# Four of eight weight pairs of an FFN panel by seven products, with x kept in DRAM between the slices

## The chip, the cores and the metric

The kernel runs on one core of a Trainium2 chip. The metric is the device time of one launch in microseconds (us). A few engines of the core matter here: TensorE (PE, the matmuls), VectorE (DVE) and ScalarE (ACT), which prepare operands and clear results, GpSimd (POOL), which before the change does next to nothing, and SyncE (SP), whose queue issues the weight loads. PEclk in a row is the share of its full clock that TensorE was granted in that stretch.

## What is computed

The reference is a model of two layers on 256 tokens of width 2048, all in fp32: a hybrid layer (a Mamba-2 scan beside attention) and a second layer with a gated delta net and sparse attention. Each ends in a feed-forward network (FFN), and the change lies in these two:

```python
x = x + mixer(rmsnorm(x, g_mix))
h = rmsnorm(x, g_mlp) @ w_up          # [256, 2048] @ [2048, 8192]
h = relu(h) ** 2
x = x + h @ w_down                    # [256, 8192] @ [8192, 2048]
```

An FFN therefore reads 128 MB of weights, each of them once.

## The kernel before

The 256 tokens are two tiles of 128. A product with fp32 operands is done as three matmuls on halves of the mantissa: high by high, high by low, low by high. So each weight has to be split: ACT copies it rounded to `whi` (L281), DVE subtracts that from the weight and gets `wlo` (L282).

`wide` (from L243) multiplies a panel of 2048 rows by 1024 weight columns. It goes through the rows in eight **pairs** j = 0 to 7; a pair is 256 rows, one weight load of 1 MB into `wst` (three buffers). A pair that is not in `spairs` is **plain**: two splits of 1024 columns on ACT and DVE, 24 matmuls of 128x512. A pair in `spairs` is done by **seven products** of a block scheme (two token tiles by two row halves, two row halves by two column halves) instead of eight: 21 matmuls, in the order P1, P3, P5, P7, P6, P4, P2. For that DVE also forms differences of weight blocks, `t13` (L303) and `t24` (L306, L307), and the splits are of three and a half 1024-wide pieces: w11 and w22, t13, t24, w21. Splits go to pools `whp` and `wlp` with four buffers each, so a split of one piece waits until PE has finished the piece four earlier.

A panel's results lie in eight PSUM banks: P2, P3, P4 and E get the direct products, P1, P5, P6, P7 the shared ones. `shared` (from L326) turns the shared ones into the four parts that have to be added to the direct banks: a copy of P1 on ACT, then P6 + P1, P5 + that, P7 + that, P5 + that on DVE (L331 to L334), 128x512 each. The next call of `wide` swaps the two groups of banks, so its first products need the banks which L331 to L334 read.

`ffn` (from L402) works in four slices of 2048 hidden columns. A slice is four panels: two **up** panels (0 and 1), whose results go through relu and square (L416 to L418), transposes on PE (L430) and splits into `hT` (L170, L172), and two **down** panels (0 and 1). For the pairs done by seven products the activations need **forms**, sums of blocks of `hT` (L232 to L235) that are split again. Down results are added by `add_blocks` (L393 to L400) to x, which lies in four SBUF tiles `X` for the whole FFN. In the last slice the second down panel is two calls of `panel` (from L183, 512 columns, splits at L207 and L208), so that x is finished in pieces.

Before the change all these panels use

```python
SPAIRS = (2, 4, 6)
```

so a panel begins with two plain pairs and ends with a plain one. The instructions of each engine run in a fixed order, which a scheduler set when the program was built; an engine waits at an instruction until what it needs is there, and what follows in its order waits with it.

## Time and profile before

| | us |
|---|---|
| median of 3 runs | 2629.16 (2626.03 to 2631.44) |
| the profiled execution | 2627.97 |
| its span in the trace | 2626.2 |
| one slice of an FFN, in the middle of it | about 171 |
| PE busy in the span | 2595.7 (99%) |
| DVE busy | 2135.3 (81%) |
| ACT busy | 1496.7 (57%) |
| POOL busy | 42.0 (2%) |

The profiled execution took 1.8 us more than its span. The panels of the two FFNs lie at about 408 to 1140 and 1935 to 2626 us of the span. Matmuls overlap in the records (one lasts 0.39 us, the next starts 0.23 us after it), so the pitch, start to start, is what one costs; the same holds for DVE and ACT. In a row of the windows view the five busy times are those of PE, of its weight loads, of DVE, ACT and POOL.

### The profile page before, as it was taken

What the parts mean: (1) busy time and instruction counts of PE and PEld (TensorE: products, weight loads), DVE (VectorE), ACT (ScalarE), POOL (GpSimd) and SP (SyncE); (2) the same over time, 40 slices, a digit from 0 to 9 for tenths busy, and PEclk for the clock granted to TensorE, in tenths of its full rate; (3) what the DMA queues carried; (4) which work ended last, traced back from release to release, by engine and by line L of the source; (5) the groups of instructions that cost most, each with busy time, mean ns of one, the idle gap of its engine ahead of it and who ended that gap; (6) DMA issues with size and microseconds to landing.
All of it is one profiled execution on the core that took longest, in us unless ns stands there. A gap on an engine that the chain in (4) does not pass through costs nothing.

```text
span 2626.2 us, 32836 instructions
## 1 busy us (share of the span) xinstructions
PE 2595.7 (99%) x12521; PEld 2165.2 (82%) x12521; DVE 2135.3 (81%) x2966; ACT 1496.7 (57%) x2006; POOL 42.0 (2%) x46
## 2 busy tenths in 40 slices
PE   8999999999999999999999999999999999999998
PEld 8998887888888888888898887888778888888886
DVE  5767789999989999676755867588999999999995
ACT  5455456656657566554533655455667566565664
POOL 0000000000000000000000000000000000000000
PEclk9999999999999999999999999999999999999999
DMA  7454555565655656753432843556455556565554
GB/s 239 143 176 157 168 178 186 182 208 197 198 198 192 194 193 196 227 184 124 133 97 87 264 165 117 177 193 224 173 196 182 203 193 208 193 207 189 197 192 160
DMA packets 181916, 478.65 MB, mean 182 GB/s; under 512 B 9127, under 2 KB 50046, under 8 KB 181758
## 3 DMA queue, kind: packets, MB, share of 16 engines
q1 hardware_dynamic: 175600, 467.57, 53.5%
q10 hardware_dynamic: 6158, 8.99, 1.0%
q8 instruction: 98, 1.61, 0.2%
q14 instruction: 60, 0.49, 0.1%
HBM read 472.32 MB, written 4.21 MB: 181 GB/s over the span
## 4 chain that ended last, share of the span: by engine, by line
PE 92%; DVE 4%; ACT 1%; DMA 1%; issue 1%; ACTq 0%; POOL 0%; POOLq 0%; SPq 0%; DVEq 0%
PE mm L270 25%; PE tp L270 13%; PE sx L270 12%; PE mm L194 10%; PE mm L193 10%; PE mm L192 10%; DVE wlo L282 2%; DMA wst<-in_w_down_dram 1%; PE sx L1021 1%; PE sx L1016 1%; ACT whi L281 1%; PE mm L430 1%; PE tp L915 0%; PE tp L369 0%; PE sx L1300 0%
## 5 line engine op out<-in xcount | busy, mean ns | idle before, releaser
L281 ACT ACTIVATE whi<-wst 128x1024 fp32r<-128x1024 f32 (+1 forms) x560 | 542.8, 979 | 312.9 <-PE mm L270 127.5
L282 DVE TENSOR_TENSOR wlo<-wst,whi 128x1024 fp32r<-128x1024 f32 (+1 forms) x560 | 615.8, 1120 | 66.1 <-ACT whi L281 63.8
L208 DVE TENSOR_TENSOR wlo<-wst,whi 128x1024 fp32r<-128x1024 f32 (+6 forms) x336 | 377.3, 1128 | 207.6 <-ACT whi L207 206.5
L207 ACT ACTIVATE whi<-wst 128x1024 fp32r<-128x1024 f32 (+6 forms) x336 | 329.2, 983 | 323.4 <-PE mm L194 294.1
L281 ACT ACTIVATE whi<-t 128x1024 fp32r<-128x1024 f32 x210 | 222.1, 1057 | 261.3 <-DVE t L307 117.0
L282 DVE TENSOR_TENSOR wlo<-t,whi 128x1024 fp32r<-128x1024 f32 x210 | 256.3, 1222 | 49.4 <-ACT whi L281 47.1
L193 PE MATMUL mm<-wlo,x2h 128*128 128x512 f32 (+3 forms) x608 | 228.3, 376 | 1.7 <-DVE wlo L208 1.7
L194 PE MATMUL mm<-whi,x2l 128*128 128x512 f32 (+3 forms) x608 | 229.7, 378 | 0.0
L192 PE MATMUL mm<-whi,x2h 128*128 128x512 f32 (+3 forms) x608 | 228.3, 376 | 0.0
L192 PE MATMUL mm<-whi,xnh 128*128 128x512 f32 (+3 forms) x416 | 152.4, 368 | 2.0 <-ACT whi L207 1.6
L270 PE MATMUL mm<-wlo,xnh 128*128 128x512 f32 x392 | 153.6, 392 | 0.4 <-DVE wlo L282 0.3
L270 PE MATMUL mm<-whi,xnl 128*128 128x512 f32 x392 | 153.1, 391 | 0.0
L270 PE MATMUL mm<-whi,xnh 128*128 128x512 f32 x392 | 151.4, 391 | 1.3 <-ACT whi L281 1.3
L193 PE MATMUL mm<-wlo,xnh 128*128 128x512 f32 (+3 forms) x416 | 151.7, 365 | 0.0
L194 PE MATMUL mm<-whi,xnl 128*128 128x512 f32 (+3 forms) x416 | 150.6, 365 | 0.1
L303 DVE TENSOR_TENSOR t<-wst 128x1024 f32<-128x1024 f32 x105 | 128.2, 1221 | 15.6 <-DMA wst<-in_w_down_dram 11.3
L270 PE MATMUL mm<-wlo,hTh 128*128 128x512 f32 x343 | 134.3, 392 | 0.8 <-DVE wlo L282 0.8
L270 PE MATMUL mm<-whi,hTl 128*128 128x512 f32 x343 | 133.6, 390 | 0.0
L270 PE MATMUL mm<-whi,hTh 128*128 128x512 f32 x343 | 132.0, 390 | 0.0
L193 PEld LDWEIGHTS mm<-wlo,x2h 128*128 128x128 f32 x608 | 114.7, 189 | 17.1 <-DVE wlo L208 2.0
L194 PEld LDWEIGHTS mm<-whi,x2l 128*128 128x128 f32 x608 | 114.5, 188 | 15.3 <-issue 1.0
L192 PEld LDWEIGHTS mm<-whi,x2h 128*128 128x128 f32 x608 | 114.7, 189 | 15.0 <-issue 0.8
(614 smaller groups left out, 5695.7 us busy)
## 6 DMA issues: line engine op xcount, KB each, us to landing
wst<-in_w_up_dram SPq DMA_DIRECT2D x128, 1024.0 KB, 5.0
wst<-in_w_down_dram SPq DMA_DIRECT2D x128, 1024.0 KB, 5.3
wst<-in_w_in_dram SPq DMA_DIRECT2D x84, 1024.0 KB, 5.1
wst<-in_w_out_dram SPq DMA_DIRECT2D x16, 1024.0 KB, 5.5
wst<-in_w_o_dram SPq DMA_DIRECT2D x16, 1024.0 KB, 5.2
wst<-in_w_in_dram SPq DMA_DIRECT2D x16, 780.0 KB, 4.5
wst<-in_w_in_dram SPq DMA_DIRECT2D x12, 824.0 KB, 4.5
wst<-in_w_in_dram SPq DMA_DIRECT2D x12, 736.0 KB, 6.2
```

Source lines behind the costliest of these rows:

```text
L192: PE.matmul(ps[t][:, :n], xh[:, sl], wa, start=kt == first, stop=False)
L193: PE.matmul(ps[t][:, :n], xh[:, sl], wb, start=False, stop=False)
L194: PE.matmul(ps[t][:, :n], xl[:, sl], wa, start=False, stop=kt == last)
L207: S.activation(a[:, :2 * n], src, AF.Copy)
L208: V.tensor_tensor(b[:, :2 * n], src, a[:, :2 * n].bitcast(F32), op=OP.subtract)
L270: PE.matmul(B[b], x, y, start=left[b] == total[b], stop=left[b] == 1)
L281: S.activation(a[:, :n], src, AF.Copy)
L282: V.tensor_tensor(b[:, :n], src, a[:, :n].bitcast(F32), op=OP.subtract)
L303: V.tensor_tensor(t13, s.rearrange("p (k l n) -> p k l n", k=2, l=2)[:, :, 0], s[:, :1024].rearrange("p (l n) -> p l n", l=2)[:, ::-1], op ...
L430: PE.transpose(pv[:, kk, t, :], us[t, l][:, c:c + 128], ident)
L1016: PE.matmul(ps[:, i * 64:(i + 1) * 64].rearrange("p (m b) -> p m b", b=b), N[:, i], half(T[:, i], 0), start=True, stop=True)
L1021: PE.matmul(ps[:, i * 64:(i + 1) * 64].rearrange("p (m b) -> p m b", b=b), P[:, i], half(Tt[:, i], 1), start=True, stop=True)
```

## The change

A second set of pairs is brought in. A panel that follows a down panel (up panel 0 of slices 1 to 3, down panel 1 of slices 0 to 2) does pairs 1, 3, 5 and 7 by seven products; the other `wide` panels of an FFN do 3, 5 and 7. x no longer stays in SBUF: it is written to DRAM (`xd`) at the FFN's start, and in the slices 0 to 2 the parts (`ca`, `cb`) and ACT's copies of the direct banks (`cd`) are added to it by DMAs issued from POOL that accumulate, four of 512 KB for a down panel. In slice 3 x is loaded back and DVE adds to it as before. The forms are now four for a slice, not three.

```diff
-    SPAIRS = (2, 4, 6)
+    SPAIRS, NPAIRS = (2, 4, 6), (1, 3, 5, 7)
...
+    def part_pairs():
+
+        return sp([128, 2, 512], name="ca"), s4([128, 2, 512], name="cb")
+
...
         for s_ in range(4):
             hT, hforms = [], {}
             for P in range(2):
-                B, tags = wide(w_up, 0, s_ * 2048 + P * 1024, at_k(act), forms, spairs=SPAIRS,
+                B, tags = wide(w_up, 0, s_ * 2048 + P * 1024, at_k(act), forms,
+                               spairs=NPAIRS[1:] if r is None or P == 1 else NPAIRS,
                                hooks={2: hook} if r is None else {})
                 us = {}
-                for i, l, part, bank in shared(B):
+                for i, l, part, bank in shared(B, part_pairs()):
...
-                        if j in SPAIRS:
-                            f = two_forms()
+                        if j in NPAIRS:
+                            f = two_forms(sp)
...
             for P in range(2):
+                if s_ == 3:
+                    for p in (2 * P, 2 * P + 1):
+                        X[p] = sp([128, 2, 512], name=f"X{p}")
+                        nc.scalar.dma_start(X[p], xd[:, p])
...
-                B, _ = wide(w_down, s_ * 2048, P * 1024, at_k(hT), hforms)
-                add_blocks(B, P)
+                B, _ = wide(w_down, s_ * 2048, P * 1024, at_k(hT), hforms, spairs=NPAIRS[1 - P:])
                 if s_ == 3:
+                    add_blocks(B, P, part_pairs())
                     for p in range(2):
                         for t in range(2):
                             after(p, t)
+                    continue
+                pairs = part_pairs()
+                out_ = shared(B, pairs)
+                banks = []
+                for l in range(2):
+                    d = sp([128, 2, 512], name="cd")
+                    for i, l_, part, bank in out_:
+                        if l_ == l:
+                            S.activation(d[:, i], bank, AF.Copy)
+                    banks.append(d)
+                for src in (pairs, banks):
+                    for l in range(2):
+                        G.dma_start(xd[:, 2 * P + 1 - l], src[l], accum_op=OP.add)
```

The lines shift by some seven to ten: L331 to L334 become L334 to L337, L397 and L400 become L404 and L407, L416 becomes L424.

Two places show what this does to the engines' orders. The first is DVE at the end of down panel 0 of the last slice in the first FFN, where `panel` follows. `wlo` at L208 is the first low half that `panel` needs; X0 and X1 are two tiles of x. Before:

```order
L331 TENSOR_TENSOR cu2_9036<-mm1_8801,cp1_9035 128x512
L208 TENSOR_TENSOR wlo_9103<-wst_9100,whi_9102 128x1024
L332 TENSOR_TENSOR cu4_9037<-mm0_8800,cu2_9036 128x512
L208 TENSOR_TENSOR wlo_9119<-wst_9100,whi_9118 128x1024
L333 TENSOR_TENSOR cu2_9036<-mm1_8802,cu2_9036 128x512
L397 TENSOR_TENSOR X0_2971<-cu4_9037,X0_2971 128x512
L334 TENSOR_TENSOR cv_9038<-mm0_8800,cu2_9036 128x512
L397 TENSOR_TENSOR X1_2972<-cu2_9036,X1_2972 128x512
L397 TENSOR_TENSOR X0_2971<-cv_9038,X0_2971 128x512
L400 TENSOR_TENSOR X1_2972<-tp_8725,X1_2972 128x512
```

After the change, on the same engine at the same place (`tp_8827` is the bank P2, the last that the panel's seven-product pair fills):

```order
L335 TENSOR_TENSOR cb_9138<-mm0_8936,ca_9137 128x512
L407 TENSOR_TENSOR X1_8825<-tp_8827,X1_8825 128x512
L336 TENSOR_TENSOR ca_9137<-mm1_8938,ca_9137 128x512
L404 TENSOR_TENSOR X0_8823<-cb_9138,X0_8823 128x512
L337 TENSOR_TENSOR cb_9138<-mm0_8936,ca_9137 128x512
L404 TENSOR_TENSOR X1_8825<-ca_9137,X1_8825 128x512
L404 TENSOR_TENSOR X0_8823<-cb_9138,X0_8823 128x512
L407 TENSOR_TENSOR X0_8823<-tp_8828,X0_8823 128x512
L407 TENSOR_TENSOR X1_8825<-sx_8829,X1_8825 128x512
L407 TENSOR_TENSOR X0_8823<-sx_8830,X0_8823 128x512
L208 TENSOR_TENSOR wlo_9207<-wst_9204,whi_9206 128x1024
```

The first two splits for `panel` stood among the sums before; now the first stands behind all of them, nine instructions after P2 is first read (that one included).

The second place is the first seven-product pair of a panel that follows an up panel, here down panel 0 of slice 2 in the first FFN. On DVE, `t13_7393` and `t24_7395` are the weight sums of that pair (pair 2). Before:

```order
L282 TENSOR_TENSOR wlo_7409<-t13_7393,whi_7408 128x1024
L172 TENSOR_TENSOR sfl_7279<-ff_7270,sfh_7278 128x512
L235 TENSOR_TENSOR ff_7296<-ff_7296 128x128
L172 TENSOR_TENSOR hTl_7290<-ff_7296,hTh_7289 128x512
L172 TENSOR_TENSOR hTl_7290<-mm1_7308,hTh_7289 128x512
L172 TENSOR_TENSOR sfl_7305<-ff_7296,sfh_7304 128x512
L282 TENSOR_TENSOR wlo_7419<-t24_7395,whi_7418 128x1024
```

After, on DVE, where that pair is pair 3 (`t13_7499`, `t24_7501`), and `t13_7577` belongs to pair 5:

```order
L306 TENSOR_TENSOR t24_7501<-wst_7493,t13_7499 128x512
L282 TENSOR_TENSOR wlo_7505<-wst_7493,whi_7504 128x1024
L172 TENSOR_TENSOR sfl_7384<-ff_7375,sfh_7383 128x512
L307 TENSOR_TENSOR t24_7501<-wst_7493,t24_7501 128x512
L282 TENSOR_TENSOR wlo_7515<-t13_7499,whi_7514 128x1024
L303 TENSOR_TENSOR t13_7577<-wst_7575 128x1024
L282 TENSOR_TENSOR wlo_7525<-t24_7501,whi_7524 128x1024
```

One more 1024-wide sum, the `t13` of the pair after next, now stands ahead of the low half of `t24`. On PE the matmuls of the same pair, after the change, from P5 on (`mm0_7496` is P5, `mm1_7498` P7, `mm1_7497` P6):

```order
L270 MATMUL mm0_7496<-whi_7514,sfh_7002 128x512
L270 MATMUL mm1_7498<-whi_7514,sfh_7002 128x512
L270 MATMUL mm1_7497<-whi_7524,sfh_7002 128x512
L270 MATMUL mm0_7496<-wlo_7515,sfh_7002 128x512
L270 MATMUL mm0_7496<-whi_7514,sfl_7003 128x512
L270 MATMUL mm1_7498<-wlo_7515,sfh_7002 128x512
L270 MATMUL mm1_7498<-whi_7514,sfl_7003 128x512
L270 MATMUL sx_7389<-whi_7524,hTh_6980 128x512
L270 MATMUL tp_7387<-whi_7534,hTh_6980 128x512
L270 MATMUL tp_7388<-whi_7543,hTh_7335 128x512
L270 MATMUL sx_7390<-whi_7543,hTh_7335 128x512
L270 MATMUL mm1_7497<-wlo_7525,sfh_7002 128x512
```

The first matmul on the low half of `t24` (the last row) is the eighteenth matmul of its pair; before the change it was the fifteenth.

## Rows read from the trace of the kernel before

**Rows 1.** The page: busy time of the engines, and the chain by engine
```profile
PE 2595.7 (99%) x12521; PEld 2165.2 (82%) x12521; DVE 2135.3 (81%) x2966; ACT 1496.7 (57%) x2006; POOL 42.0 (2%) x46
...
PE 92%; DVE 4%; ACT 1%; DMA 1%; issue 1%; ACTq 0%; POOL 0%; POOLq 0%; SPq 0%; DVEq 0%
```

**Rows 2.** Windows, one slice each: stretch, length, busy (instructions), PEclk, DMA share, GB/s
```profile
453.00:625.00 172.00, 171.72 (x769) 140.63 (x768) 158.44 (x189) 103.83 (x122) 0.00 (x0) 1.00 0.60 198
...
2184.50:2355.00 170.50, 170.25 (x765) 140.12 (x764) 157.24 (x188) 104.34 (x122) 0.00 (x0) 1.00 0.57 198
```

**Rows 3.** Chain in order of time: start, length, what, how many
```profile
2294.54 6.80 PE mm L270 x30
```

**Rows 4.** Timeline, first up panel, first FFN, PE: start, length, what, [idle before <-releaser]
```profile
418.35 0.40 PE L270 MATMUL tp<-whi,sfh 128*128 128x512 f32 x1
420.32 0.73 PE L270 MATMUL mm<-whi,sfh 128*128 128x512 f32 x2 [1.57 <-DVE sfl L172]
422.07 0.50 PE L270 MATMUL mm<-whi,sfh 128*128 128x512 f32 x1 [1.01 <-ACT whi L281]
...
426.09 0.40 PE L270 MATMUL mm<-whi,sfl 128*128 128x512 f32 x1
```

**Rows 5.** Windows of that place, and of the last panels of the second FFN
```profile
417.50:426.20 8.70, 6.11 (x19) 4.12 (x19) 7.83 (x12) 4.96 (x7) 1.07 (x1) 0.80 0.02 9
...
2572.50:2576.50 4.00, 4.00 (x13) 3.10 (x12) 3.10 (x5) 1.36 (x5) 0.00 (x0) 0.57 0.79 261
```

**Rows 6.** Timeline, first up panel of the second FFN, PE
```profile
1941.50 0.50 PE L270 MATMUL mm<-wlo,xnh 128*128 128x512 f32 x1 [0.29 <-DVE wlo L282]
```

**Rows 7.** Timeline, up panel to down panel, slice 2, first FFN, DVE
```profile
832.20 1.23 DVE L282 TENSOR_TENSOR wlo<-wst,whi 128x1024 fp32r<-128x1024 f32 x1 [1.09 <-ACT whi L281]
...
841.54 2.35 DVE L282 TENSOR_TENSOR wlo<-wst,whi 128x1024 fp32r<-128x1024 f32 x2
843.80 1.22 DVE L303 TENSOR_TENSOR t<-wst 128x1024 f32<-128x1024 f32 x1
...
854.17 1.22 DVE L282 TENSOR_TENSOR wlo<-t,whi 128x1024 fp32r<-128x1024 f32 x1
```

**Rows 8.** The same place, PE
```profile
829.55 0.39 PE L270 MATMUL tp<-whi,xnh 128*128 128x512 f32 x1
...
852.62 0.39 PE L270 MATMUL mm<-whi,hTh 128*128 128x512 f32 x1
...
855.79 0.39 PE L270 MATMUL mm<-wlo,sfh 128*128 128x512 f32 x1
```

**Rows 9.** Timeline, down panel to up panel, first FFN, PE
```profile
586.81 0.50 PE L270 MATMUL mm<-whi,xnh 128*128 128x512 f32 x1 [0.24 <-ACT whi L281]
```

**Rows 10.** Timeline, end of down panel 0, slice 3, first FFN, DVE
```profile
1052.83 1.22 DVE L208 TENSOR_TENSOR wlo<-wst,whi 128x1024 fp32r<-128x1024 f32 x1
...
1056.96 1.28 DVE L400 TENSOR_TENSOR X<-tp,X 128x512 f32<-128x512 f32 x2
```

**Rows 11.** The same place, PE
```profile
1055.09 0.39 PE L192 MATMUL mm<-whi,hTh 128*128 128x512 f32 x1
```

**Rows 12.** Timeline, the same end in the second FFN, DVE
```profile
2571.01 2.48 DVE L400 TENSOR_TENSOR X<-mm,X 128x512 f32<-128x512 f32 x4
```

**Rows 13.** The same place, PE
```profile
2568.89 0.39 PE L270 MATMUL mm<-whi,hTl 128*128 128x512 f32 x1
...
2571.85 0.47 PE L192 MATMUL mm<-whi,hTh 128*128 128x512 f32 x1 [2.57 <-DVE X L400]
...
2572.85 0.54 PE L193 MATMUL mm<-wlo,hTh 128*128 128x512 f32 x1
...
2576.18 0.48 PE L192 MATMUL mm<-whi,hTh 128*128 128x512 f32 x1
```

**Rows 14.** DMA issues: tile<-source, queue, kind, how many, KB each, median us to landing
```profile
wst<-in_w_down_dram SPq DMA_DIRECT2D x128, 1024.0 KB, 5.3
...
xsave<-X ACTq DMA_DIRECT2D x4, 512.0 KB, 5.6
```

More of the change, by code (lines that the diff above doesn't have):

```diff
@@ L219, in panel, with two_forms @@
         return ps
-    SPAIRS = (2, 4, 6)
+    SPAIRS, NPAIRS = (2, 4, 6), (1, 3, 5, 7)
     turn = [0]
-    def two_forms():
-        f = s4([128, 2, 512], name="ff")
+    def two_forms(pool=s4):
+        f = pool([128, 2, 512], name="ff")
         return f[:, 0].rearrange("p (k t c) -> p k t c", k=2, t=2), f[:, 1].rearrange("p (f c) -> p f c", f=4)
@@ L325, in wide, with shared @@
         return B, ka
-    def shared(B):
-        p1, u2, u4, v = (s2([128, 512], name=n) for n in ("cp1", "cu2", "cu4", "cv"))
+    def shared(B, pairs=None):
+        if pairs is None:
+            p1, u2, u4, v = (s2([128, 512], name=n) for n in ("cp1", "cu2", "cu4", "cv"))
+        else:
+            (p1, u2), (u4, v) = ((t[:, 0], t[:, 1]) for t in pairs)
         S.activation(p1, B["P1"], AF.Copy)
@@ L369, in x_to_act @@
                     PE.transpose(ps[:, kk, t, :], x[:, t, (k0 + kk) * 128:(k0 + kk + 1) * 128], ident)
-            if forms is not None and 2 * p + k0 // 2 in SPAIRS:
+            if forms is not None and 2 * p + k0 // 2 in NPAIRS:
                 f = two_forms()
@@ L391, in flat, with add_blocks @@
         return ap.rearrange("p k c -> p (k c)")
-    def add_blocks(B, P):
-        out_ = shared(B)
+    def part_pairs():
+        return sp([128, 2, 512], name="ca"), s4([128, 2, 512], name="cb")
+    def add_blocks(B, P, pairs=None):
+        out_ = shared(B, pairs)
         for i, l, part, bank in out_:
@@ L400, in add_blocks, with ffn @@
             V.tensor_tensor(x, bank, x, op=OP.add)
-    def ffn(act, forms, w_up, w_down, late, after, tail=0):
+    def ffn(act, forms, xd, w_up, w_down, late, after, tail=0):
         r = None
@@ L451, in ffn @@
                             after(p, t)
+                    continue
+                pairs = part_pairs()
+                out_ = shared(B, pairs)
+                banks = []
[8 more added lines that the diff above has]
+                        G.dma_start(xd[:, 2 * P + 1 - l], src[l], accum_op=OP.add)
     ssx = tiny([128, 2, 4], "ssx", bufs=2)
@@ L824, in x_done @@
             sumsq(ssx[:, t, p:p + 1], X[p][:, t])
+        nc.scalar.dma_start(xd[:, p], X[p])
     X = x_panels()
     xforms = {}
+    xd = drp.tile([128, 4, 2, 512], F32, name="xd")
     for p in range(4):
@@ L852, in after1 @@
             nc.scalar.dma_start(xsave[:, p], X[p])
-    ffn(xn, xforms, I["w_up"][0], I["w_down"][0], late1, after1)
+    ffn(xn, xforms, xd, I["w_up"][0], I["w_down"][0], late1, after1)
     if upto == 2:
@@ L1376, in build @@
     xforms = {}
+    xd = drp.tile([128, 4, 2, 512], F32, name="xd2")
     ssx = tiny([128, 2, 4], "ssx", bufs=2)
@@ L1416, in after2 @@
         nc.sync.dma_start(o[:, 1024:1536], X[2][:, t])
-    ffn(xn, xforms, I["w_up_2"][0], I["w_down_2"][0], late2, after2, tail=8)
+    ffn(xn, xforms, xd, I["w_up_2"][0], I["w_down_2"][0], late2, after2, tail=8)
 _INS = ["x", "g_mix", "w_in", "conv_w", "conv_b", "dt_bias", "a_log", "d_skip", "g_ssd", "g_q", "g_k", "g_kidx",
```

## The prediction

> **What bounds the kernel now.** I read the page first: PE is busy for 99% of the span and makes up 92% of the chain, DVE is next with 81% [rows 1]. In the middle of an FFN it is tighter still: PE is busy for 171.7 of 172.0 us at full clock, DVE for 158.4, ACT for 103.8, and the DMA engines are used to 0.60 [rows 2]. So two things follow. Matmuls taken away are time taken away, one for one, where nothing else becomes late. And little more than the matmuls can be gained inside a slice, since PE stands still for under 1 us in it; whereas DVE, with 13 us to spare in 171, can become late at any place where its work is bunched. The question is therefore not the load of DVE but what stands in its order ahead of a half that PE needs.
>
> Prices, all pitches: a matmul 6.80/30 = 0.2267 us [rows 3]; a 1024-wide DVE operation 1.13 (two in 2.35, one alone 1.22) [rows 7]; a 512-wide one 0.60 (four in 2.48, two in 1.28) [rows 10, 12]. A plain pair is then 24 x 0.2267 = 5.44 us of PE and 2.26 of DVE; a pair by seven products 4.76 of PE and 4 x 1.13 + 3 x 0.60 = 6.3 of DVE.
>
> **Matmuls removed.** Six panels of each FFN have four instead of three such pairs: 2 x 6 x 3 = 36 matmuls fewer, 36 x 0.2267 = **-8.2 us**, all on the path.
>
> **DVE's load.** A slice gets two more such pairs (2 x 4.0 = +8), loses sixteen additions to x (-9.6) and gains one form (about +1.4). It stays near 157 us. So what counts is the places.
>
> **First up panels.** In the first up panel of an FFN the first pair by seven products was 2 and is now 3, so 5.44 us of plain work cover the wait for its form. Now PE waits 1.57 us for the form and 1.01 for a high half [rows 4], and the clock is 0.80 over the stretch [rows 5]: from 418.35 to 426.09 thirteen matmuls start, worth 2.9 us, so 4.8 are lost. In the second FFN a wait of 0.29 is marked [rows 6], with some more around it. DVE has one more form to make ahead of it. I take 2 and 1: **-3 us**, bounds -1 and -6.
>
> **Up panel to next panel** (sixteen times). All panels of an FFN done by `wide` now end with pair 7 by seven products, and a panel after an up panel then has three plain pairs and pair 3. Before, it was pair 6, plain 7, 0, 1 and pair 2: the same PE work from one such pair to the next, 852.62 - 829.55 = 23.1 us [rows 8]. DVE starts this stretch 2.65 us after the pair's start (832.20) and is never idle for long until the low half of `t24` at 854.17 + 1.22 = 855.39 [rows 7]; PE uses that at 855.79 [rows 8]. It is on time by 0.40 us. After the change the list from the first shared sum to that half is the same, sixteen 512-wide and eight 128-wide operations, but ten 1024-wide ones and not nine (`t13` of pair 5 is put ahead): +1.13. PE's order for its part uses the half three matmuls later, +0.68 of cover. Late by 1.13 - 0.40 - 0.68 = 0.05 us. That is the floor: the three matmuls moved ahead need high halves from ACT at that moment, and every bubble in DVE's chain (transposes, copies, forms, handed to and fro with ACT and PE) now comes on top, without slack. If the cover doesn't work it is 0.73, with bubbles 0.9. I take 0.4: 16 x 0.4 = **+6.4 us**, bounds 0 and 14.
>
> **Down panel to next panel** (twelve times). The next panel's products need the banks that the four shared sums read; a plain pair 7 used to cover these. Now, from the start of pair 7: 2.65 us to DVE's first split, then three 1024-wide and five 512-wide operations to the last sum, 2.65 + 3.4 + 3.0 = 9.05. PE has 4.76 of pair 7 and, with P2 and P4 of pair 0 put first and E next, 18 matmuls (4.1) ahead of P3, 8.84: late by 0.2 to 0.4. The gap there now is 0.24 as marked [rows 9]. Net 0.12 each, **+1.5 us**, bounds 0 and 4. The sixteen fewer additions to x lie behind these sums and free nothing earlier. ACT's 48 copies of direct banks and the splits behind them fit in its 68 idle us of a slice [rows 2]; I cost them at nothing, and at 0.5 us each where ACT is late, which the upper bound holds.
>
> **End of down panel 0 in slice 3** (once in each FFN). Here DVE still adds to x, and `panel` comes next. Before, its first low halves were made between the sums (1052.83), the additions of banks came later (1056.96) [rows 10], and PE went on at 1055.09 with no idle marked [rows 11]. Now nine 512-wide additions and sums stand between the first reading of P2 and `wlo`. P2 is complete 4.76 us after the start of pair 7, read from 4.96: 4.96 + 9 x 0.60 = 10.4, with the split 11.5. PE has done 4.76 + 0.45 by then, and 0.9 of transposes of x that it has to do anyway: it waits 5.4. In the second FFN it waits already: from 2568.89 + 0.23 to 2571.85, 2.7 us, for the additions [rows 12, 13]. There the low half comes one operation later still, 12.1: a wait of about 6.9, so +4.2. After its wait that place ran at 0.57 of the clock [rows 5]: eight matmuls in 3.33 us and not 1.81, 1.5 lost [rows 13]; the first FFN gets that new, the second perhaps 0.4 more. 5.4 + 4.2 + 1.5 + 0.4 = **+11.5 us**, bounds 7 (the sums start early, no loss of clock) and 15 (a longer low clock).
>
> **Accumulating DMAs.** The trace has none. A down panel's four of 512 KB are 2 MB beside 8 MB of weights. A copy of 512 KB from SBUF to DRAM lands in 5.6 us, a load of 1 MB in 5.3 [rows 14]. At the price of plain bytes the share rises from 0.60 [rows 2] to 0.75, and the three weight buffers hide it; full it is at 2.7 times that price. Nothing on POOL waits behind them, and their sources are needed again 25 us and more later (by the panel lengths). Value 0, bounds 0 and the third rival.
>
> The Trainium skill has a rule that speaks against this: "Collectives: The Full Stack", section "The bandwidth ceiling: the fold count and why AG ≠ RS ≠ AR", says that an adding transfer reads two sources for each write, and gives 32 against 62 GB/s. By that rule the share here would be about 0.90 (an estimate), which leaves the sum as it is but brings the third rival near; no run here shows it yet.
>
> **The sum**: -8.2 - 3 + 6.4 + 1.5 + 11.5 = +8.2. The profiled execution took 2627.97 us, so 2636.2; the median of the three runs is 1.2 above it, within their spread of 5. I predict 2636.
>
> **Rivals.** (1) *Not slower: DVE stays ahead after every panel.* PE's later use of the low halves suffices, and both transition terms are 0: 2628.0 - 8.2 - 3 + 11.5 = 2628. For it: 0.05 us is all that the count shows. Against: no slack is left. It decides at 0.1 us of bubbles in a transition. (2) *Faster: the wait in slice 3 is short as well*, because DVE takes up most sums before P2 is complete: its lower bound 7, the first up panels' full 6, no transition cost: 2628.0 - 8.2 - 6 + 7 = 2621. For it: the same sums were started early before (1052.83) [rows 10]. Against: PE completes P6 and P2 only at the panel's end now. (3) *The additions fill the DMA engines.* At three times the price of plain bytes the share in a down panel would be 0.60 x 1.75 = 1.05, so 5% of 43 us, 2.1 us for each of twelve: 2636 + 26 = 2662; at four times 2740. For it: the weights in the same engines. Against: 0.40 is free.
>
> **How the numbers follow.** Chances: forecast 0.53, (1) 0.27, (2) 0.10, (3) 0.10. The sum of all lower bounds is -8, of all upper ones +24; so 2621 to 2652, with a little for the third rival 2654. A measurement of this kernel tells about 0.2%, 5.3 us, from no change. Faster than that: rival 2 and the edge of 1, 0.12. Within: most of 1 and the low side of the forecast, 0.28. Slower: 0.60.
>
> **What would show it.** PE's busy time down by about 8 us. In slice 3 a wait of some 5 us for `wlo` of L208 in the first FFN and some 7 in the second, each followed by matmuls at 0.43 us. After up panels, waits of 0.1 to 0.9 us for `wlo` from `t24` in pair 3; slices near 171 us still. DMA share near 0.68 in the slices 0 to 2. Wrong it would be if slices were shorter by 1.4 us and the two ends cost nothing, or if weight loads became what DVE and ACT wait for.

## The result: slower by 2.3%, and where the time went

| kernel | median, us | ratio to the kernel before (95% interval) | profiled span, us |
|---|---|---|---|
| before | 2629.16 (2626.03 to 2631.44, 5 runs) | | 2626.2 |
| after | 2688.22 (2685.22 to 2692.92, 5 runs) | 1.0226 [1.0214, 1.0237] | 2684.5 |

Slower was forecast, but by 8, not by 59; the time lies outside the range of 2621 to 2654.

The page of the changed kernel first: its span, the busy times, the share of each engine in the chain of work that ended last, the queue of DMAs issued from POOL (packets, MB, share of 16 engines' span), and some DMA issues (count, KB each, median us to landing; the last two lines are from the DMA view).

```profile
span 2684.5 us, 33032 instructions
PE 2612.6 (97%) x12485; PEld 2153.5 (80%) x12485; DVE 2138.8 (80%) x2978; ACT 1555.9 (58%) x2098; POOL 82.6 (3%) x94
...
q0 software_dynamic: 6912, 25.17, 5.3%
...
PE 63%; DVE 20%; DMA 9%; ACT 5%; issue 3%; ACTq 0%; POOL 0%; POOLq 0%; DVEq 0%; SPq 0%
...
wst<-in_w_up_dram SPq DMA_DIRECT2D x128, 1024.0 KB, 5.1
wst<-in_w_down_dram SPq DMA_DIRECT2D x128, 1024.0 KB, 5.5
...
xd<-cd POOLq DMA_DIRECT2D x24, 512.0 KB, 10.1
...
xd<-ca POOLq DMA_DIRECT2D x12, 512.0 KB, 6.7
xd<-cb POOLq DMA_DIRECT2D x12, 512.0 KB, 8.3
```

PE made up 92% of the chain before [rows 1] and makes up 63% now; DVE and the DMAs stand where it stood. DVE does hardly more than before. The weight loads land in the same median time as before [rows 14], which hides a few that take twice as long. An adding DMA of 512 KB takes 6.7 to 10.1 us in the median.

A slice of the first and one of the second FFN, as in [rows 2] (us, the five busy times, PEclk, DMA share, GB/s):

```profile
618.20:797.30 179.10, 173.37 (x758) 138.02 (x758) 156.84 (x187) 112.83 (x137) 6.92 (x8) 1.00 0.69 212
...
2165.20:2342.00 176.80, 172.43 (x758) 138.27 (x758) 156.94 (x187) 113.07 (x137) 6.92 (x8) 1.00 0.68 215
```

A slice took 172.0 and 170.5 and takes 179.1 and 176.8, at full clock and with the DVE load that the prediction gave (157). PE now stands still for 4 to 6 us of it. The mean DMA share of 0.69 looks harmless.

To see which panels pay, take the start of each panel's first matmul from the trace of the profiled execution, and the time to the next one. Means in us; the last two columns run from the start of down panel 0 of slice 3 to the next layer's first `wide` panel (first FFN) and to the last matmul (second FFN):

| | after a down panel (12) | up panel 1 (8) | down panel 0 (6) | first up panels (2) | end, FFN 1 | end, FFN 2 |
|---|---|---|---|---|---|---|
| before | 42.10 | 43.50 | 43.47 | 48.13, 46.33 | 693.7 | 91.6 |
| after | 44.07 | 45.07 | 45.22 | 43.47, 44.17 | 701.2 | 101.1 |
| difference, all | +23.7 | +12.6 | +10.5 | -6.8 | +7.5 | +9.5 |

That is +57.0 of the +58.3 of span. The panels after a down panel are the surprise: three matmuls fewer should have made them 0.68 shorter, and they are 1.97 longer.

### The profile page after: what moved, and what is told of

It is laid out like the page before. It is cut to its first block, busy times and chain, and to the rows that moved or that the text cites. A ratio compares the mean times of both kernels' runs of the same rounds, so it can differ in the third digit from the quotient of the medians.

```text
span 2684.5 us, 33032 instructions
## 1 busy us (share of the span) xinstructions
PE 2612.6 (97%) x12485; PEld 2153.5 (80%) x12485; DVE 2138.8 (80%) x2978; ACT 1555.9 (58%) x2098; POOL 82.6 (3%) x94
## 3 DMA queue, kind: packets, MB, share of 16 engines
q0 software_dynamic: 6912, 25.17, 5.3%
## 4 chain that ended last, share of the span: by engine, by line
PE 63%; DVE 20%; DMA 9%; ACT 5%; issue 3%; ACTq 0%; POOL 0%; POOLq 0%; DVEq 0%; SPq 0%
PE mm L270 12%; PE mm L194 10%; PE mm L193 10%; PE mm L192 10%; DVE wlo L282 10%; PE tp L270 6%; PE sx L270 6%; DMA wst<-in_w_down_dram 4%; DMA wst<-in_w_up_dram 4%; ACT whi L281 3%; DVE t L303 2%; DVE hTl L172 1%; DVE t L307 1%; DVE t L306 1%; DVE sfl L172 1%
## 5 line engine op out<-in xcount | busy, mean ns | idle before, releaser
L282 DVE TENSOR_TENSOR wlo<-wst,whi 128x1024 fp32r<-128x1024 f32 (+1 forms) x560 | 609.2, 1109 | 83.3 <-ACT whi L281 81.5
L281 ACT ACTIVATE whi<-wst 128x1024 fp32r<-128x1024 f32 (+1 forms) x560 | 535.3, 969 | 230.1 <-PE mm L270 70.7
L208 DVE TENSOR_TENSOR wlo<-wst,whi 128x1024 fp32r<-128x1024 f32 (+6 forms) x336 | 377.2, 1128 | 209.2 <-ACT whi L207 208.3
L281 ACT ACTIVATE whi<-t 128x1024 fp32r<-128x1024 f32 x234 | 247.7, 1059 | 322.0 <-DVE t L307 206.0
L282 DVE TENSOR_TENSOR wlo<-t,whi 128x1024 fp32r<-128x1024 f32 x234 | 284.4, 1222 | 48.0 <-ACT whi L281 44.6
L303 DVE TENSOR_TENSOR t<-wst 128x1024 f32<-128x1024 f32 x117 | 142.8, 1221 | 52.5 <-DMA wst<-in_w_down_dram 27.6
L270 PE MATMUL mm<-wlo,xnh 128*128 128x512 f32 x377 | 148.2, 393 | 2.4 <-DVE wlo L282 2.4
L270 PE MATMUL mm<-whi,xnl 128*128 128x512 f32 x377 | 147.4, 391 | 0.0
L270 PE MATMUL mm<-whi,xnh 128*128 128x512 f32 x377 | 143.4, 393 | 0.5 <-DVE ca L336 0.5
L270 PE MATMUL mm<-whi,hTl 128*128 128x512 f32 x328 | 127.9, 390 | 0.0
L270 PE MATMUL mm<-whi,hTh 128*128 128x512 f32 x328 | 126.2, 394 | 0.5 <-DVE ca L336 0.5
## 6 DMA issues: line engine op xcount, KB each, us to landing
xd<-cd POOLq DMA_DIRECT2D x24, 512.0 KB, 10.1
```

The lines of the kernel that those rows point to most:

```text
L208: V.tensor_tensor(b[:, :2 * n], src, a[:, :2 * n].bitcast(F32), op=OP.subtract)
L270: PE.matmul(B[b], x, y, start=left[b] == total[b], stop=left[b] == 1)
L281: S.activation(a[:, :n], src, AF.Copy)
L282: V.tensor_tensor(b[:, :n], src, a[:, :n].bitcast(F32), op=OP.subtract)
L303: V.tensor_tensor(t13, s.rearrange("p (k l n) -> p k l n", k=2, l=2)[:, :, 0], s[:, :1024].rearrange("p (l n) -> p l n", l=2)[:, ::-1], op ...
```

## The experiments

**The adding DMAs.** Three kernels leave the changed kernel's panels as they are and change the DMAs alone. The first leaves the 48 adding DMAs out (so x lacks the down panels of slices 0 to 2); the second moves the same bytes without adding (each overwrites what was there).

```diff
                 for src in (pairs, banks):
                     for l in range(2):
-                        G.dma_start(xd[:, 2 * P + 1 - l], src[l], accum_op=OP.add)      # noacc: all three lines out
+                        G.dma_start(xd[:, 2 * P + 1 - l], src[l])                       # plain
```

> The changed kernel without its 48 accumulating DMAs (the sums of the slices 0 to 2 are left out of x; all sums, copies and loads stay). Theory A: for some 20 us after each down panel the adding DMAs, whose 4 KB packets took 327 ns and not 159, starve the weight loads; the twelve panels that follow a down panel then lose about 2.4 us each. Without them these panels return to 41 to 42 us from 43.3 to 45.5, and the time to 2688 - 29 = about 2659. Theory B: the order of DVE (a panel that ends with a pair by seven products, sums of weights put early) makes the loss: the time stays within 8 us of 2688.

> The changed kernel with the 48 DMAs as plain writes of the same bytes (they overwrite x's copy and do not add to it). Theory A, with the price of adding as its core: packets take 159 ns again, the share of the DMA engines in a slice falls from 0.69 to 0.64, most of the loss goes: about 2665. If any extra traffic at that place starves the loads, at whatever price: 2675 to 2685. Theory B: 2688.

Measured: 2652.32 without them (1.0094 [1.0077, 1.0111]) and 2657.30 with plain copies (1.0110 [1.0095, 1.0125]). So some 31 of the 59 us belong to the adding. That the bytes cost anything isn't shown: the two intervals overlap, and in the profiled executions the difference lies in the stretch of the table's column "end, FFN 1" (700.4 and 705.7), where no such DMA runs. Panels after a down panel take 41.51 and 41.52 us, against 42.10 before and 44.07 after: the saving of the three matmuls is there once the adding is gone. The POOL queue and the issues of `plain`:

```profile
q0 software_dynamic: 6912, 25.17, 2.4%
...
xd<-cd POOLq DMA_DIRECT2D x24, 512.0 KB, 6.1
```

The price of adding follows from the two shares: 0.053 x 16 x 2684.5 / 6912 = 0.329 us for a packet in the mean, against 0.024 x 16 x 2655.7 / 6912 = 0.148 us for a plain one, 2.2 times (768 of the 6912 carry 4 bytes; the packets of 4 KB took 0.365 and 0.164 us in the mean). The four DMAs of a panel occupy all sixteen engines for 0.053 x 2684.5 / 12 = 11.9 us. Spread over a panel that would fit, so the question is when they run. POOL's timeline in the panel from 719 on in the first FFN (start, us, what; in brackets the idle time before it and what ended it):

```profile
723.01 0.86 POOL L476 DMA_DIRECT2D xd<-ca  x1 [124.49 <-issue]
724.00 0.86 POOL L476 DMA_DIRECT2D xd<-cb  x1
730.08 0.86 POOL L476 DMA_DIRECT2D xd<-cd  x1 [5.22 <-DMA xd<-ca]
732.63 0.86 POOL L476 DMA_DIRECT2D xd<-cd  x1 [1.68 <-DMA xd<-cb]
```

The two DMAs of the parts go at once, and each of the two of the banks as soon as the one that adds to the same half of the panel's columns has landed. The last one lands at 743, so additions are under way for 20 us (20 to 22 in all twelve panels). The same panel and the next one as windows of the changed kernel (columns as above):

```profile
720.00:745.00 25.00, 24.82 (x110) 20.24 (x109) 21.51 (x24) 14.27 (x17) 3.46 (x4) 1.00 1.01 276
745.00:750.00 5.00, 3.98 (x17) 2.69 (x15) 3.79 (x6) 2.59 (x4) 0.00 (x0) 1.00 0.39 161
765.00:790.00 25.00, 24.82 (x109) 19.92 (x108) 20.88 (x23) 13.19 (x15) 3.46 (x4) 1.00 1.03 283
790.00:795.00 5.00, 3.89 (x15) 2.33 (x14) 3.79 (x6) 2.93 (x4) 0.00 (x0) 1.00 0.13 53
```

For 25 us the engines are full (1.01, 1.03), and PE is still busy throughout; it loses a fifth of the 5 us after that, when the engines are at 0.39 and 0.13. This is how a late load appears: PE lives on the buffers while the engines are full, and stands still when they have run out. What the two queues get (packets, MB, share of the window) from 735 to 741, with both at work, and then from 743 to 746, with the additions done; and a weight load issued at 772, in the next burst:

```profile
q0 software_dynamic: 214, 0.81, 67.6%
q1 hardware_dynamic: 211, 0.86, 37.9%
...
q1 hardware_dynamic: 328, 1.28, 103.7%
...
wst<-in_w_up_dram SPq DMA_DIRECT2D x1, 1024.0 KB, 9.7
```

Beside the additions the packets of the two queues come about one for one (214 and 211), and as the adding ones take longer the weights move 0.86 MB in 6 us, a third of the rate that they have alone (1.28 MB in 3 us). The load issued at 772 lands after 9.7 us, not 5.1. The wait then goes down the line. The same kernel's timeline behind the first burst, one row each from DVE, ACT and three from PE (columns as in POOL's, with engine and line):

```profile
742.87 1.22 DVE L303 TENSOR_TENSOR t<-wst 128x1024 f32<-128x1024 f32 x1 [2.19 <-DMA wst<-in_w_down_dram]
```

```profile
742.88 1.06 ACT L281 ACTIVATE whi<-wst 128x1024 fp32r<-128x1024 f32 x1 [3.46 <-DMA wst<-in_w_down_dram]
```

```profile
748.79 0.49 PE L270 MATMUL sx<-whi,sfh 128*128 128x512 f32 x1 [0.31 <-ACT whi L281]
750.05 0.50 PE L270 MATMUL sx<-wlo,sfh 128*128 128x512 f32 x1 [0.77 <-DVE wlo L282]
...
752.93 0.50 PE L270 MATMUL mm<-wlo,hTh 128*128 128x512 f32 x1 [0.54 <-DVE wlo L282]
```

DVE and ACT wait for the weights of pair 5, and 6 us later PE waits for their halves: 1.62 us marked, in a panel that takes 43.77 us where `noacc` takes 41.55.

The third kernel keeps the additions and only spaces them: the two of the parts go as before, the two of the banks after `t13` of pair 5 of the next panel, by a one-column POOL copy of it ahead of them in POOL's queue.

```diff
+            if held and j == 5:
+                g = G.tensor_copy(tiny([128, 1], "gate"), t13[:, 0, 0:1])
+                with tc.issue_after(g.ins):
+                    for dst, src in held:
+                        G.dma_start(dst, src, accum_op=OP.add)
...
+                    held.append((xd[:, 2 * P + 1 - l], banks[l]))
```

> The changed kernel with the same bytes, packets and order of adding DMAs, but with the two that add the direct banks held back on POOL's queue until the weight sum of pair 5 of the next panel is made, some 20 us later. Theory A in its sharp form (it is the burst of four that starves the loads, not the mean share of 0.69): the panels after a down panel lose half as much, 2688 - 15 = 2673. If the total of the traffic counts, the time stays within 5 us of 2688.

Measured: 2657.67 (1.0113 [1.0099, 1.0127]), as good as plain copies; its panels after a down panel take 41.57 us. The row of the POOL queue, POOL's timeline and two stretches of the same panel (it begins at 714 here):

```profile
q0 software_dynamic: 6912, 25.17, 5.5%
```

```profile
718.27 0.86 POOL L482 DMA_DIRECT2D xd<-ca  x1 [109.84 <-issue]
719.26 0.87 POOL L482 DMA_DIRECT2D xd<-cb  x1
737.21 1.05 POOL L307 COPY gate<-t 128x1 f32<-128x1 f32 x1 [17.09 <-DVE t L304]
738.20 1.75 POOL L310 DMA_DIRECT2D xd<-cd  x2
```

```profile
712.00:737.00 25.00, 24.82 (x110) 20.20 (x109) 23.23 (x26) 16.17 (x19) 1.73 (x2) 1.00 0.83 235
737.00:757.00 20.00, 19.96 (x88) 16.24 (x87) 17.19 (x20) 12.48 (x14) 2.74 (x3) 1.00 0.91 281
```

The additions cost the engines as much as before (5.5% of 16 x 2656.8 us, 0.338 us a packet), but the share stays at 0.83 and 0.91, and PE is busy for 19.96 of 20 us where it stood still. So it is the burst that costs the 31 us: the second two additions on the heels of the first two (7 to 9 us after them in this panel, 19 to 20 in the spaced kernel). Neither their price nor their bytes decide by themselves.

**Half of the additions.** DVE adds the direct banks to the parts again, and only two DMAs are left for a panel.

```diff
-                banks = []
+                for i, l, part, bank in out_:
+                    V.tensor_tensor(part, bank, part, op=OP.add)
...
-                for src in (pairs, banks):
-                    for l in range(2):
-                        G.dma_start(xd[:, 2 * P + 1 - l], src[l], accum_op=OP.add)
+                    G.dma_start(xd[:, 2 * P + 1 - l], pairs[l], accum_op=OP.add)
```

> The changed kernel with DVE adding the four direct banks to the parts (four 512-wide operations for a down panel), so that two adding DMAs of 512 KB go out for a down panel and not four, and ACT copies no banks. Theory A: half the burst, 5 us of all engines and not 10, is taken up by the three weight buffers: the twelve panels after a down panel go from 44.2 to about 42, less some 0.5 us for DVE's 2.4 us more: 2688 - 22 = 2666. Rival (what counts is that such DMAs run at all): 2680 and more.

Measured: 2668.63 (1.0158 [1.0141, 1.0175]): 20 of the 31 us back, at the price of DVE's additions; 42.78 us for a panel after a down panel.

**Down panel 0.** In slices 0 to 2 it has no adding DMA ahead of it, yet takes 1.75 us more, in `noacc` too (45.46). Its wait, in the timeline of the changed kernel, DVE and then PE:

```profile
885.29 1.23 DVE L303 TENSOR_TENSOR t<-wst 128x1024 f32<-128x1024 f32 x1 [2.33 <-DMA wst<-in_w_down_dram]
886.44 2.36 DVE L282 TENSOR_TENSOR wlo<-wst,whi 128x1024 fp32r<-128x1024 f32 x2
```

```profile
887.71 0.50 PE L270 MATMUL tp<-wlo,hTh 128*128 128x512 f32 x1 [1.28 <-DVE wlo L282]
```

DVE stands at `t13` of pair 7, whose weights are not there, with the splits of pair 6, whose weights are, queued behind it. To see whether that order is the cause, one kernel ties each `t13` to the last low half written ahead of it in the program:

```diff
-            V.tensor_tensor(t13, ...
+            with tc.issue_after(lastlo[0].ins):
+                V.tensor_tensor(t13, ...
```

> The changed kernel with one rule on DVE's order: the weight sum t13 of a pair is not queued ahead of the last low half of the pair before. Theory C: the panels after an up panel (44.4 and 45.7 us, 43.5 before) lose 1.6 us each because a t13 put early blocks DVE until its load lands (waits of 1.5 to 2.3 us in front of t13 of pair 7) or takes the slot of a half that PE needs (pair 3). Then these fourteen panels go to about 43.7 and the time to 2688 - 18 = 2670, with the adding DMAs' loss left in the panels after a down panel. Rival: they lose because the bursts of adding DMAs reach into them; then nothing moves by more than 5 us.

Measured: 2674.77 (1.0180 [1.0165, 1.0195]), 13 us better than after. Down panel 0 takes 43.98, so 1.24 of its 1.75 are this order; from 880 to 892 no idle of PE is marked any more. Up panel 1 goes from 45.07 to 44.52.

**The end of down panel 0 in slice 3.** One kernel does pairs 1, 3, 5 there, so that a plain pair 7 covers the sums; another makes the first four splits for `panel` ahead of the sums.

```diff
-                B, _ = wide(w_down, s_ * 2048, P * 1024, at_k(hT), hforms, spairs=NPAIRS[1 - P:])
+                B, _ = wide(w_down, s_ * 2048, P * 1024, at_k(hT), hforms, spairs=(1, 3, 5) if s_ == 3 else NPAIRS[1 - P:])     # s3
...
+                    pre = list(splits4(w_down, s_ * 2048, 1024, 512))                                                       # pre3
```

> The changed kernel, with down panel 0 of slice 3 alone doing pairs 1, 3 and 5 by seven products and so ending with two plain pairs. The place lost 16.9 us in all, of which I put 11.5 on the sums that stand ahead of the low halves of the next panel. If so, 2688 - 11 = about 2677, and the waits at the end of that panel (4.1 and 1.0 us in the first FFN; 1.0, 3.9 and 2.1 in the second) go down to what stood there before. If the loads of x from DRAM make the loss at that place, it stays within 3 us of 2688.

> The changed kernel with the load and the two splits of the first rows of the panel that follows down panel 0 in slice 3 written ahead of the additions to x, so that DVE makes these two low halves before the nine operations. Theory (my prediction's step): the wait at that place (4.1 + 1.0 us and a half-clock stretch in the first FFN; 1.0 + 3.9 + 2.1 and half clock in the second, where a bank has to be freed as well) goes in the first FFN and shrinks to that of the kernel before in the second: 2688 - 12 = 2676. Rival: the banks or the transposes of x are what PE waits for there: within 4 us of 2688.

Measured: 2688.73 for pairs 1, 3, 5 (1.0232 [1.0215, 1.0249]) and 2679.33 for the early splits (1.0197 [1.0182, 1.0212]). The first takes away the end waits and buys one of the same size in pair 1, since DVE makes its `t13` only behind the forms, whose last split ends at 1043.69, and PE waits for the high half of it (PE's timeline of that kernel):

```profile
1046.05 1.22 PE L270 MATMUL mm<-whi,sfh 128*128 128x512 f32 x2 [6.00 <-ACT whi L281]
```

The second takes most of the end waits away and gives 9 us back, so the order there is a cause; in the second FFN a wait of 2.98 us for an addition to x stays.

**Three edits at once** (half the additions, the order of `t13`, the early splits):

> The three edits together (half as many adding DMAs, t13 not put early, first splits of the next panel ahead of the additions in slice 3). If the three causes are separate, their gains add up: 2688 - 22 - 18 - 12 = 2636; with the 8.2 us of matmuls and some 7 us of the first up panels all kept, 2620 to 2640. If they are not separate (one late chain seen at three places), the sum is reached by one of them and this run gives no more than the best single one.

Measured: 2674.51 (1.0181 [1.0163, 1.0199]), no better than the order of `t13` alone and worse than half of the additions alone. The gains don't add up. Two reasons show. The rule that helps down panel 0 puts `t13` of pair 1 behind the split of pair 0, and in each of the twelve panels after a down panel PE now waits for a low half behind it, 1.03 us at 548.67 and 1.02 at 592.29, and 0.58 more for a high half; these panels take 44.31. And at the end of slice 3 of the second FFN PE waits 6.1 us for an addition to x.

**Other pairs.** The change's two halves apart: first the old pairs 2, 4, 6 with x in DRAM, then pairs 3, 5, 7 in all `wide` panels of an FFN with x in SBUF, as before.

```diff
-    SPAIRS, NPAIRS = (2, 4, 6), (1, 3, 5, 7)
+    SPAIRS, NPAIRS = (2, 4, 6), (2, 4, 6)        # p246, from the changed kernel; every panel takes NPAIRS
...
-    SPAIRS = (2, 4, 6)
+    SPAIRS, FPAIRS = (2, 4, 6), (3, 5, 7)        # p357, from the kernel before; every panel of an FFN takes FPAIRS
```

> The changed kernel with the pairs of before (2, 4, 6) in all panels of the FFN; x in DRAM and the adding DMAs stay. Theory A: the loads are late after each down panel here too, so 12 x 2 us stay, and the up transitions, the first up panels and the ends in slice 3 are as before: about 2650 to 2655. Theory B: all of the loss goes: 2627 to 2634.

> The kernel before with pairs 3, 5 and 7 by seven products in all wide panels of both FFNs; x stays in SBUF, no adding DMA, no fourth form, no fewer matmuls. If the order alone makes the rest of the loss (panels after an up panel about 1 and 2 us longer, the ends in slice 3 about 12, the first up panels 7 shorter), this takes 2629 + 14 x 1.3 + 12 - 7 = about 2650. If x in DRAM is behind the rest, it stays within 8 us of 2629.

Measured: 2749.75 for the old pairs with x in DRAM (1.0460 [1.0442, 1.0479]), far off what was expected: moving x alone costs twice as much as the whole change. With pairs 2, 4, 6 it is `t13` of pair 4 that meets the late load, and it stands in DVE's order ahead of the low half of pair 2's `t24`, whose high half is ready at 742.83. The waits list of that kernel (engine, line, waited for: us in total, times, longest), where `t13` waits for the weights, one of these waits, and what PE then waits:

```profile
DVE t L303 <- DMA wst<-in_w_down_dram: 62.5, 25, 7.5
DVE t L303 <- DMA wst<-in_w_up_dram: 49.2, 13, 8.1
```

```profile
748.85 1.23 DVE L303 TENSOR_TENSOR t<-wst 128x1024 f32<-128x1024 f32 x1 [7.48 <-DMA wst<-in_w_down_dram]
```

```profile
752.00 0.60 PE L270 MATMUL sx<-wlo,sfh 128*128 128x512 f32 x1 [4.64 <-DVE wlo L282]
```

In the changed kernel the two totals are 27.6 and 23.3 us, and `t13` of pair 5 waited 2.19 in the rows above. A panel after a down panel takes 48.39 here. Behind this wait PE runs at the lower clock for a while (0.79 in the mean from 752 to 760); the mean granted clock of the span is 0.984 against 0.996, up to some 33 us of the 122 (an estimate, 0.012 x 2751). So what the burst makes of the time depends on which instruction DVE meets in it.

Pairs 3, 5, 7 with x in SBUF took 2647.47 (1.0073 [1.0059, 1.0086]). Panels after an up panel are as long as before (43.54, 43.54). Panels after a down panel are 1.55 longer, for another reason, which DVE and PE of that kernel show:

```profile
718.15 1.27 DVE L400 TENSOR_TENSOR X<-sx,X 128x512 f32<-128x512 f32 x2
719.35 2.35 DVE L282 TENSOR_TENSOR wlo<-wst,whi 128x1024 fp32r<-128x1024 f32 x2
```

```profile
720.62 0.50 PE L270 MATMUL mm<-wlo,hTh 128*128 128x512 f32 x1 [1.86 <-DVE wlo L282]
```

Without a plain pair 7 the eight additions to x stand ahead of the low halves of the next panel's second pair. Moving them to DMAs removes this wait; the burst is what came in its place.

**From the changed kernel to a better one?** Spaced additions, the order of `t13` for pairs 3, 5 and 7 only, early splits, and the two groups of banks swapped once in the second layer:

> The changed kernel with four edits: the two DMAs of direct banks held back by some 20 us, t13 of the pairs 3, 5 and 7 not put ahead of the halves of the pair before, the first splits of the next panel ahead of the additions in slice 3, the groups of banks swapped once in the second layer. If the causes are the ones named and separate: 2658 (held back) - 13 (dn0 panels 45.7 to 43.8) - 9 (ends) - 3 = 2633, about level with before, the 8 us of matmuls being used up by the 1 us that each second up panel still loses and by the end in slice 3. If some other cost of x in DRAM remains: over 2645.

Measured: 2638.67 (1.0042 [1.0026, 1.0057]): 50 of the 59 us back, and still not as fast as before.

**From the kernel before.** Only the first up panels gained more than predicted, and this gain needs neither x in DRAM nor a fourth pair. In the kernel before, pair 3 can simply be done ahead of pair 2 there:

```diff
                 B, tags = wide(w_up, 0, s_ * 2048 + P * 1024, at_k(act), forms, spairs=SPAIRS,
+                               order=(0, 1, 3, 2, 5, 4, 7, 6) if r is None else range(8),      # first, tog1, tog2
+                               order=(0, 1, 3, 2, 4, 5, 6, 7) if r is None else range(8),      # good
+                               order=(0, 1, 3, 2, 5, 4, 6, 7) if r is None else range(8),      # good2
...
+    turn[0] += 1      # swap the groups of banks once in the second layer: tog2, good, good2; 29 lines further on: tog1
```

> The kernel before with one edit: in the first up panel of each FFN the pairs are worked through in the order 0, 1, 3, 2, 5, 4, 7, 6, so that a plain pair stands ahead of the first one by seven products, as the change has it there. In the changed kernel these two panels were 4.7 and 2.2 us shorter. If that is due to the plain pair ahead, this is faster than before by 4 to 7 us, less up to 2 us since the panel now ends with a pair by seven products: 2622 to 2626. If it came from the other edits, it is 2629 or more.

> The same as the run named first, and the two groups of banks are swapped once ahead of the last projection of the second layer, so that the end of down panel 0 in the last slice of the second FFN meets the bank groups as the first FFN does. There the kernel before waited 2.7 us for the additions to x, with 1.5 us of half clock after it. If the bank group is the cause, another 4 us go, less up to 3 us where two calls in a row use the same group: 2618 to 2624.

> As the run named tog1, with the swap placed one projection earlier, where plain panels stand ahead of it. The wait at the end of the second FFN should go as there (4 us less than first); the swap itself should cost less or nothing: 2617 to 2622. If it is not faster than the run named first, the wait at that place does not come from the bank group.

> The kernel before with the first up panel of each FFN in the order 0, 1, 3, 2, 4, 5, 6, 7 and the bank groups swapped once in the second layer. The first panels' 4.6 and 2.7 us stay, and no panel ends with a pair by seven products; two such pairs in a row cost up to 1.5 us in each: 2629 - 7 + 2 - 3 = 2621. If the gain is given back in the panels that follow in any case, 2627 to 2631.

> As the run named good, with the order 0, 1, 3, 2, 5, 4, 6, 7, so that the two neighbouring pairs by seven products are the last but one and the last but two. Same gain if the panel's end is what counts (2621); worse than good by 1 to 3 us if the two pairs in a row make the low halves late right ahead of the panel's end.

| | median, us | ratio (95% interval) | first up panels | end, FFN 2 |
|---|---|---|---|---|
| before | | | 48.13, 46.33 | 91.6 |
| first | 2631.81 | 1.0012 [1.0003, 1.0021] | 43.53, 43.67 | 91.6 |
| tog1 | 2630.14 | 1.0006 [0.9997, 1.0015] | 43.51, 43.67 | 88.6 |
| tog2 | 2629.97 | 1.0003 [0.9995, 1.0012] | 43.50, 44.29 | 88.6 |
| good | 2623.16 | 0.9979 [0.9970, 0.9988] | 46.42, 44.25 | 89.0 |
| good2 | 2618.75 | 0.9961 [0.9949, 0.9974] | 44.01, 43.65 | 88.8 |

The kernel before took 2629.53 beside the first three and 2628.17 beside the last two. The first order has its 7 us in the first panels and gives them back behind, in slice 0: up panel 1 there takes 45.01 and 44.44 (43.62 and 43.49 before), down panel 1 takes 46.05 and 46.01 (42.14 and 42.06), where a low half stands behind the additions to x. The last order, which ends with the plain pair 7, keeps them (43.44 and 43.66; 42.77 and 41.65). Why the order of one panel changes DVE's order further on stays open. The bank swap takes 3 us off the end of the second FFN. The last order and the swap together make a kernel 0.4% faster than before and 2.6% faster than after. The stretch of [rows 5] in it, somewhat wider:

```profile
410.00:440.00 30.00, 30.00 (x134) 24.16 (x132) 29.59 (x43) 19.59 (x32) 3.94 (x1) 1.00 0.55 196
```

PE is busy for all of it, at full clock.

## Why the prediction failed, step by step

The panels sum to +57: some 31 are the additions (forecast 0), 23 the panels after an up panel (forecast 6.4 with the two of slice 3), 17 the ends (11.5), -6.8 the first up panels (-3); the matmuls and the panels after a down panel, without the additions, came as forecast. So the sign of the forecast was right, but the largest term was not in its sum.

**Accumulating DMAs: the step that failed.** It took value 0 because the share in a down panel, averaged over the panel, stayed under one up to 2.7 times the price of plain bytes. The price was 2.2 times, below that point, and the step still cost some 31 us: the average was the wrong measure. The four DMAs follow each other closely after a down panel, the engines are full for over 20 us, and the three buffers don't cover a weight load's delay (9.7 instead of 5.1 us). The sign that the prediction chose, a share near 0.68 in a slice, came out (0.69 and 0.68) and told nothing; its sign of being wrong came true: `t13` waits 27.6 and 23.3 us for weight loads, 11.3 and 3.1 before. The third rival named the right mechanism with the wrong condition. The rule of the Trainium skill on adding transfers ("Collectives: The Full Stack", "The bandwidth ceiling: the fold count and why AG ≠ RS ≠ AR"; 32 against 62 GB/s), stated there for a ReduceScatter against an AllGather, gave a price near that measured: 62/32 is 1.9, the packets here show 2.2. The estimate made from it, a mean share of 0.90, would still not have told the loss.

**Down panel to next panel** (+1.5 in all). Taken by itself it was right: in `noacc` these panels take 41.51, and 42.10 - 0.68 + 0.12 = 41.54. What was missed is the 2.5 us each of the burst.

**The additions to x "free nothing earlier".** Wrong. In `p357` they stand ahead of the low half that PE needs and cost 1.86 us there. That these twelve panels are short in `noacc` goes with taking them away.

**Up panel to next panel** (0.4 each, 16 times). Mis-sized: +1.57 for each up panel 1 and +1.75 for each down panel 0, 23 us in all for the fourteen of the table. Most of the latter is the order of `t13` of pair 7, which was not looked for: the prediction followed the start of the next panel only, not its end. For the former, `p357`, with pair 3 first too but one form less after up panel 0 and x in SBUF, loses nothing (43.54); which of the two matters there is not shown. The marked waits are small, as forecast, but for a high half and not for the low half of `t24`:

```profile
648.98 0.50 PE L270 MATMUL sx<-whi,sfh 128*128 128x512 f32 x1 [0.30 <-ACT whi L281]
```

What makes up the 1.57 was not settled: the adding DMAs of the panel before have their part (44.76 without them, 44.58 spaced), and so has the order of `t13` (44.52). Up panel 1 of slice 0 loses most, 2.5 and 2.7 us.

**First up panels** (-3, bounds -1 and -6). Right in kind, too small, with the sum beyond the bound: -4.7 and -2.2. The stretch of [rows 5] now has no idle time at all, so the whole 4.8 us that the prediction had counted as lost came back, where it took 2 and 1.

```profile
417.50:426.20 8.70, 8.70 (x39) 6.97 (x38) 8.64 (x14) 6.37 (x11) 3.94 (x1) 1.00 0.44 147
```

**End of down panel 0 in slice 3** (+11.5, bounds 7 and 15). The waits are where and nearly as long as predicted. PE in the first FFN, then in the second, and the clock behind it:

```profile
1080.97 0.44 PE L372 MATMUL tp<-idt,X 128*128 128x128 f32 x2 [3.93 <-DVE X L407]
1082.17 1.54 PE L372 MATMUL tp<-idt,X 128*128 128x128 f32 x6 [0.76 <-DVE X L407]
```

```profile
2623.49 0.47 PE L192 MATMUL mm<-whi,hTh 128*128 128x512 f32 x1 [0.88 <-DVE X L407]
2627.59 0.55 PE L192 MATMUL mm<-whi,hTh 128*128 128x512 f32 x1 [3.63 <-DVE X L407]
2629.92 0.79 PE L193 MATMUL mm<-wlo,hTh 128*128 128x512 f32 x1 [1.78 <-DVE wlo L208]
```

```profile
2630.00:2634.80 4.80, 4.80 (x12) 3.75 (x13) 4.80 (x6) 0.67 (x3) 0.00 (x0) 0.51 0.16 21
```

4.69 us in the first (5.4 predicted) and 6.29 in the second (6.9), ended by the additions to x as well as by the low half. Behind the second, ten matmuls run at the lower clock (0.51); in the first FFN the clock is at 0.50 from 1082 to 1084. The term came to +17 in all, beyond its bound of 15: the same panel has one more wait in each FFN, of 2.28 and 2.56 us (at 1051.42 and 2596.45), where DVE stands at `t13` of pair 5, whose weights are not there, ahead of work of pair 3. `nohoist` shows that this too is mainly the order of `t13`: in it there are two short waits instead, 0.61 and 0.25 in the first FFN, 0.60 and 0.24 in the second. Why the load is late there, with the loads of x beside it, stays open.

**Matmuls removed and DVE's load.** The 36 matmuls are gone and slices hold 157 us of DVE, as predicted. PE's busy time went up, not down by 8 (2612.6 against 2595.7), so it was of no use as a check. The records overlap (0.39 us long, 0.23 apart), so a delay of up to 0.16 us leaves no idle time and counts as busy; and a matmul behind a wait has a longer record, 0.49 us at 748.79.

**The range.** The lower bounds add up to -7.2, not to -8; the 2621 made from them holds.

Not tried: a fourth weight buffer, which would test directly how much delay the three cover.

## What to carry to other kernels

A new DMA stream has to be costed in the window in which it is issued, against what is buffered there, not as a mean share over a stage: four transfers that fit easily into a panel stopped PE in it by coming on each other's heels, and spacing them was worth as much as making them half as dear. Where an in-order engine prepares operands, look at what the new order puts ahead of each load that may be late, at the end of the stage as well as at its start. And try the part of a change that gains by itself: the order of one panel, with no x in DRAM, made a kernel faster than either of the two, together with one swap of banks.

## What the chip showed that was not expected

A packet of 4 KB of a DMA that adds from SBUF to DRAM took 0.365 us in the mean, a plain one 0.164. With additions and weight loads queued together, their packets came one for one (214 and 211 in 6 us), so the weights moved at a third of the rate that they have alone. A load of 1 MB issued in such a stretch landed in 9.7 us instead of 5.1.
